# A hybrid encoder trunk: one projection of the recurrent layer and the value projection of the attention layer change their place in two order strings

## Chip, cores and metric

The kernel runs on one core of one Trainium2 chip. The metric is device time in microseconds (us); the time before is the median of three runs, 1386.49 us (1385.02 to 1387.21).

## The reference, cut to what matters

Sequence 512, width 1024, one batch, two layers. Each layer adds three blocks to x: a mixer, a cross-attention into 256 memory tokens, and a SwiGLU feed-forward network with 2816 hidden units.

```
layer 0 mixer: h = rmsnorm(x);  h @ w_in gives q, k, v, z (4 delta-rule heads) and xb, gb (512 channels)
    delta rule in chunks of 64 over q, k, v;  o = rmsnorm(o) * silu(z)
    xb = causal_conv4(xb) + b;  r, i = sigmoid(block_diag(xb));  a = exp(-8 r softplus(-l))
    hs = scan(a, sqrt(1 - a^2) * i * xb);  y_b = gelu(gb) * hs;  concat(y_a, y_b) @ w_out
layer 1 mixer: h @ w_in gives qc, kc, vc (4 differential heads, two softmaxes each), q_lat, kv_lat, k_rope
    qd, kd, vd from the latents (4 latent heads, rotary part);  both kinds of heads attend chunk-causally
    concat(yc, yd) @ w_out
```

All is float32. A product of two float32 matrices is made by three matmuls on values split into a high part and a low part (`mm3`, line 454): high times high, high times low, low times high, each in the fast float32r format. Score, transpose and probability matmuls use plain float32.

## The kernel before, in words

The activations lie transposed, 128 features by 512 positions a tile, and all 8 tiles of x stay in SBUF. Each weight tile (128 x 1024) is loaded by the SP queue into one of three raw buffers, its high part is written by ScalarE or VectorE (`wh`, line 368 or 363), its low part by VectorE (`wl`, line 385), each into one of three buffers; a projection of a 128-feature tile is then 24 matmuls of 512 columns (8 k-tiles, three products each).

The program does not issue as it is written. Every operation goes into a plan (`Plan.add`), where its rank is its place in the program plus a small bias, and `Plan.schedule` deals the operations to the engines one after another with a cost table: on each engine it takes, of those that can start within 20 ns (TensorE) or 60 ns (others) of the earliest, the one with the lowest rank. So TensorE fills every wait with something of higher rank if its operands are ready. A copy that either ScalarE or VectorE can make goes where it ends sooner. PSUM has eight banks, all under the tag `ps`; SBUF scratch has 70 slots; an operation may take a bank only when enough stay free for those of lower rank that still wait. The issue order that comes out is fixed in the program; the chip then waits on semaphores.

The ranks come from two strings. `EVEN` (line 1490) is layer 0's mixer. The letters around the change: `R` is the delta-rule recurrence (`recur`), `x0` to `x3` project and convolve the channel tiles (`xhead`, line 1038: 24 matmuls, a multiply by the norm factor into `cx`, one scale and three shifted multiply-adds into `cv`), `g0` to `g3` project the gate tiles (`ghead`, line 1044: 24 matmuls and the multiply into `gb`; gelu comes in `L`), `W` loads the block-diagonal weights, `L` (`lru`, line 1071) makes 8 float32 matmuls on the four `cv` tiles, sigmoids, the scan, gelu and the split into `ybhh`, `ybhl`, `z` are the gates of the delta-rule heads, `N` its norm, `F` the filler, which is layer 0's memory keys and values (`mem_kv`, line 645), and `Y` the last step of the delta-rule heads.

`ODD` (line 1491) is layer 1's mixer: `L` the latent projection, `K` and `Q` the key and query projections of the differential heads (`natural_heads`, line 1376: 96 matmuls into four banks, then for each of four position tiles an eviction into `xn`, a square, a sum, and after one reciprocal root a multiply), `N` the latent norm, `V` their value projection (`values`, line 1403: 96 matmuls into four banks and four evictions into `vc`, four weight tiles), `U` the up-projections of the latents (`latent_up`, line 1285), `R` the rotary part and key norms (`rope`), `D0` to `D3` the latent heads (`mla`, line 1354), `C0` to `C3` the differential heads (`diff`, line 1410), `F` layer 1's memory keys and values: 96 matmuls, in eight weight tiles of 12 matmuls each, two banks at a time. The C heads read `vc`; the D heads read `vd` of `U` and not `vc`.

Ahead of this lies layer 0's feed-forward network and behind it the output projection, which needs all eight heads.

Of the kernel before, what the change touches and what calls it, by code (L numbers as in the profile page):

```python
# [20 lines left out]
D, S, NM, FF = 1024, 512, 256, 2816  # L21
# [279 lines left out]
class Trunk:  # L301
# [465 lines left out]
    def even(self, filler):  # L767
# [333 lines left out]
        def gated(h):  # L1101
            pT = self.px()
            for t in range(4):
# [9 lines left out]
               "z": zhead, "Y": gated}  # L1113
        for name in EVEN.split():
            self.mark[name] = len(self.plan.ops)
# [115 lines left out]
    def odd(self, filler):  # L1231
# [178 lines left out]
        def diff(h):  # L1410
            ck, cq = pairT(g["od_k"], h, self.cqk[:, h:h + 1]), pairT(g["od_q"], h, 1.0)
            slope = 2.0 ** (-8.0 * (h + 1) / 4)
            P = []
            for t in range(4):
                n = 128 * (t + 1)
                sl = slice(t * 128, (t + 1) * 128)
                pr, sm = [], self.small([128, 2], "smm")
                rows = [slice(i * 64, i * 64 + 64) for i in range(2)]
                sc = [self.px()[:, :n] for _ in rows]
                self.mmpair(sc, [cq[r, sl] for r in rows], [ck[r, :n] for r in rows])  # L1420
                for i in range(2):
                    p = self.slot("P")
                    mx = self.small([128, 1], "mx")
                    self.submax(p[:, :n], sc[i], self.dist[t][:, :n], mx)
                    self.ts(mx, mx, -slope, ALU.mult)
                    self.act(p[:, :n], p[:, :n], AF.Exp, scale=slope, bias=mx, accum_out=sm[:, i:i + 1])
                    pr.append(p)
                self.recip(sm, sm)
                self.mul(sm[:, 1:2], sm[:, 1:2], self.lam)
                self.ts(pr[1][:, :n], pr[1][:, :n], sm[:, 1:2], ALU.mult)  # L1430
                self.stt(pr[0][:, :n], pr[0][:, :n], sm[:, 0:1], pr[1][:, :n], ALU.mult, ALU.subtract)
                P.append(pr[0])
            po = self.pv(P, vc, h)
            y = self.scr("yc")
            sq = self.scr("ysq")
            self.act(sq, po, AF.Square)
            cs = self.px()
            self.mm(cs, self.ones, sq)
            self.rsqrt_wide(sq, cs, 1.0 / 128, self.eps)
            self.stt(y, po, self.csub, sq, ALU.mult, ALU.mult)  # L1440
            a, b = self.pair("ych")
            self.split(a, b, y)
            yk[h] = (a, b)
# [3 lines left out]
        for i in range(4):  # L1447
            todo[f"D{i}"] = lambda i=i: mla(i)
            todo[f"C{i}"] = lambda i=i: diff(i)
        for name in ODD.split():  # L1450
            todo[name]()
# [35 lines left out]


LATE = {"norm_mix0": 30, "norm_mix1": 30, "norm_x0": 0, "norm_x1": 0, "norm_ffn0": 40, "norm_ffn1": 40, "gate": 40, "consts": 200}
EVEN = "k0 k3 k1 k2 A q3 I T0 q2 T1 T2 v1 q1 q0 T3 T4 P T5 S v2 v0 V0 V1 V2 v3 V3 R x0 g0 x3 x1 g2 g1 x2 g3 W L z0 z2 z1 N z3 F Y"  # L1490
ODD = "L K N Q V U R D3 D0 C1 C2 D1 C0 C3 D2 F"
HOLD = ("T0", "R")
NSLOT = 70
WRAW = 3
# [92 lines left out]
```

## Time and profile before

| | |
|---|---|
| median of three runs | 1386.49 us |
| the profiled execution, its time | 1383.43 us |
| its span, first to last instruction | 1381.6 us |
| granted TensorE clock over the span | 1.000 |
| TensorE matmul busy | 1369.6 us, 99% |
| TensorE weight loads busy | 1124.8 us, 81% |
| VectorE busy | 824.3 us, 60% |
| ScalarE busy | 563.0 us, 41% |

A matmul's end in the trace is modelled, and consecutive matmuls overlap, so the busy time of TensorE counts stretches as full in which the matmuls stand further apart than they need. What a stretch had to do is read from the counts of its matmuls and the distance of their starts where they stand densest.

### The profile page before, as it was taken

To read this page: it belongs to the slowest core of one execution; us is meant where nothing else is said; L and a number is where in the kernel's file an instruction comes from. 1 tells how busy PE (TensorE), PEld (TensorE's weight loads), DVE (VectorE), ACT (ScalarE), POOL (GpSimd) and SP (SyncE) were. 2 spreads that over 40 slices of the span, in tenths; PEclk is the share of its full clock that TensorE was granted. 3 is DMA by queue.
4 is the path that set the end of the run, shared out by engine and by line. 5 is a ranking of instruction groups with operands and counts; after the bars stand their busy time and mean duration, and the time that the engine had idled before them with its cause. 6 is when DMAs were issued, how large, how long until landed. Compare 5 with 4: busy or idle time off the path is not lost.

```text
span 1381.6 us, 18085 instructions
## 1 busy us (share of the span) xinstructions
PE 1369.6 (99%) x7212; PEld 1124.8 (81%) x7212; DVE 824.3 (60%) x1474; ACT 563.0 (41%) x998; POOL 3.0 (0%) x10
## 2 busy tenths in 40 slices
PE   9999999999999999999999999999999999999998
PEld 7788787888888888888889885688888888888887
DVE  7988877867744433544454469976774443344432
ACT  5763438425533222333233357843652222233221
POOL 0000000000000000000000000000000000000000
PEclk9999999999999999999999999999999999999999
DMA  6121121531232223332233220132122322422232
GB/s 241 55 86 47 48 75 35 179 95 61 76 105 92 88 90 118 125 104 83 84 101 110 96 73 31 31 135 94 46 92 92 106 70 93 128 92 92 88 107 80
DMA packets 40692, 125.89 MB, mean 91 GB/s; under 512 B 4896, under 2 KB 5536, under 8 KB 40608
## 3 DMA queue, kind: packets, MB, share of 16 engines
q1 hardware_dynamic: 40608, 124.74, 27.9%
q8 instruction: 56, 0.92, 0.3%
q14 instruction: 28, 0.23, 0.1%
HBM read 122.63 MB, written 2.10 MB: 90 GB/s over the span
## 4 chain that ended last, share of the span: by engine, by line
PE 96%; DVE 3%; ACT 1%; issue 0%; DVEq 0%
PE ps L434 91%; PE ps L440 3%; PE ps L470 2%; PE ps L450 1%; DVE gt L385 0%; ACT P L368 0%; DVE gt L418 0%; DVE cv L400 0%; DVE wl L385 0%; ACT sq L368 0%; DVE ybhl L385 0%; DVE kn L363 0%; DVE cT L365 0%; DVE kn L385 0%; ACT PT L368 0%
## 5 line engine op out<-in xcount | busy, mean ns | idle before, releaser
L368 ACT ACTIVATE wh<-wr 128x1024 fp32r<-128x1024 f32 (+3 forms) x218 | 212.3, 974 | 628.0 <-PE ps L434 421.0
L434 PE MATMUL ps<-hh,wl 128*128 128x512 f32 x960 | 375.8, 392 | 0.3 <-DVE wl L385 0.3
L434 PE MATMUL ps<-hh,wh 128*128 128x512 f32 x960 | 376.1, 392 | 0.0
L434 PE MATMUL ps<-hl,wh 128*128 128x512 f32 x960 | 375.8, 391 | 0.0
L385 DVE TENSOR_TENSOR wl<-wr,wh 128x1024 fp32r<-128x1024 f32 (+3 forms) x243 | 272.9, 1124 | 120.8 <-ACT wh L368 120.1
L434 PEld LDWEIGHTS ps<-hl,wh 128*128 128x128 f32 x960 | 180.3, 188 | 38.4 <-issue 1.5
L434 PEld LDWEIGHTS ps<-hh,wl 128*128 128x128 f32 x960 | 180.3, 188 | 38.0 <-issue 0.7
L434 PEld LDWEIGHTS ps<-hh,wh 128*128 128x128 f32 x960 | 180.2, 188 | 37.9 <-issue 0.9
L434 PE MATMUL ps<-ghh,wh 128*128 128x512 f32 x352 | 136.9, 389 | 0.0
L434 PE MATMUL ps<-ghl,wh 128*128 128x512 f32 x352 | 136.9, 389 | 0.0
L434 PE MATMUL ps<-ghh,wl 128*128 128x512 f32 x352 | 136.9, 389 | 0.0
L385 DVE TENSOR_TENSOR up<-ps,R 128x512 f32<-128x512 f32 x44 | 30.4, 691 | 139.6 <-PE ps L434 139.6
L385 DVE TENSOR_TENSOR x<-x,ps 128x512 f32<-128x512 f32 x56 | 37.9, 687 | 80.6 <-PE ps L434 80.4
L385 DVE TENSOR_TENSOR gate<-ps,R 128x512 f32<-128x512 f32 x44 | 30.4, 691 | 90.5 <-PE ps L434 89.9
L434 PEld LDWEIGHTS ps<-ghl,wh 128*128 128x128 f32 x352 | 66.1, 188 | 13.8
L434 PEld LDWEIGHTS ps<-ghh,wh 128*128 128x128 f32 x352 | 66.1, 188 | 13.8
L434 PEld LDWEIGHTS ps<-ghh,wl 128*128 128x128 f32 x352 | 66.1, 188 | 13.6
L434 PE MATMUL ps<-wh,hl 128*128 128x512 f32 (+1 forms) x128 | 49.0, 383 | 0.0
L434 PE MATMUL ps<-wl,hh 128*128 128x512 f32 (+1 forms) x128 | 48.7, 380 | 0.0
L434 PE MATMUL ps<-wh,hh 128*128 128x512 f32 (+1 forms) x128 | 48.6, 380 | 0.0
L1485 ACT ACT_TABLE_LOAD x28 | 35.9, 1283 | 1.2 <-PEq L1569 0.7
L400 DVE SCALAR_TENSOR_TENSOR cv<-cx,vcols,cv 128x511 f32<-128x511 f32 (+2 forms) x48 | 35.8, 745 | 0.3
(388 smaller groups left out, 1829.5 us busy)
## 6 DMA issues: line engine op xcount, KB each, us to landing
wr<-in_ffn_in_dram SPq DMA_DIRECT2D x88, 512.0 KB, 3.5
wr<-in_ffn_out_dram SPq DMA_DIRECT2D x32, 384.0 KB, 3.0
wr<-in_ev_in_dram SPq DMA_DIRECT2D x20, 512.0 KB, 3.5
wr<-in_ffn_out_dram SPq DMA_DIRECT2D x32, 320.0 KB, 2.8
wr<-in_xwk_dram SPq DMA_DIRECT2D x8, 512.0 KB, 3.5
wr<-in_xwv_dram SPq DMA_DIRECT2D x8, 512.0 KB, 3.7
wr<-in_ev_out_dram SPq DMA_DIRECT2D x8, 512.0 KB, 3.5
wr<-in_xwq_dram SPq DMA_DIRECT2D x8, 512.0 KB, 3.5
```

The source lines that it names most:

```text
L368: self.plan.add(ACT, lambda: self.nc.scalar.activation(out, in_, f, **k), outs, ins, self.acost(in_, len(ins) + len(outs) - 2), "tanh" if ...
L385: self.dve(lambda: self.nc.vector.tensor_tensor(out, a, b, op=op), [out], [a, b])
L400: self.dve(lambda: self.nc.vector.scalar_tensor_tensor(out, a, s, b, op0=op0, op1=op1), [out], [a, b] + sc, 1.0, len(sc))
L434: self.plan.add(PE, lambda: self.nc.tensor.matmul(ps, l, r, start=start, stop=stop, **k), [ps], [l, r], cost, None, n * (1 if l.dtype == F ...
L440: self.nc.tensor.matmul(out, l, r, start=True, stop=True)
L450: self.nc.tensor.matmul(ps[i], l[i], r[i], start=True, stop=True)
L470: self.plan.add(PE, lambda: self.nc.tensor.transpose(out, in_, i), [out], [in_, i], 109.0, None, in_.shape[0])
L1485: self.nc.scalar.preload_act_table_set(pre)
```

## The change

Two ranks move. In `EVEN`, `x2` comes ahead of `g2` and `g1` in place of behind them. In `ODD`, `V` leaves its place between `Q` and `U` and comes behind `D3` and `D0`, and `C1 C2 D1 C0 C3 D2` becomes `C1 D1 C2 D2 C0 C3`. No operation is added, removed or resized.

```
-EVEN = "... V3 R x0 g0 x3 x1 g2 g1 x2 g3 W L z0 z2 z1 N z3 F Y"
-ODD = "L K N Q V U R D3 D0 C1 C2 D1 C0 C3 D2 F"
+EVEN = "... V3 R x0 g0 x3 x1 x2 g2 g1 g3 W L z0 z2 z1 N z3 F Y"
+ODD = "L K N Q U R D3 D0 V C1 D1 C2 D2 C0 C3 F"
```

## Rows read from the trace of the kernel before

**Rows 1.** The page: busy time of each engine, and the chain that ended last by engine.
```profile
PE 1369.6 (99%) x7212; PEld 1124.8 (81%) x7212; DVE 824.3 (60%) x1474; ACT 563.0 (41%) x998; POOL 3.0 (0%) x10
PE 96%; DVE 3%; ACT 1%; issue 0%; DVEq 0%
```

**Rows 2.** The timeline of TensorE in the dense stretch of the value projection, first and last of 73 consecutive matmuls (start us, us, engine, line, operation, names, shapes, count).
```profile
799.82 0.39 PE L434 MATMUL ps<-wh,hl 128*128 128x512 f32 x1
...
816.14 0.39 PE L434 MATMUL ps<-wh,hl 128*128 128x512 f32 x1
```

**Rows 3.** The same view, where plain float32 matmuls, transposes and the paired scores of a C head stand in a run, each with the instruction behind it.
```profile
206.63 7.03 PE L434 MATMUL ps<-cv,gbd 128*128 128x512 f32 x16
...
213.72 0.40 PE L434 MATMUL ps<-hl,wh 128*128 128x512 f32 x1
...
771.52 1.47 PE L470 MATMUL ps<-consts,latn 128*128 128x128 f32 x12
772.74 0.48 PE L434 MATMUL ps<-wh,hh 128*128 128x512 f32 x1
773.06 0.39 PE L434 MATMUL ps<-wl,hh 128*128 128x512 f32 x1
...
848.23 0.70 PE L450 MATMUL ps<-cT,cT 64*128 64x256 f32 x4
848.86 0.33 PE L470 MATMUL ps<-consts,P 128*128 128x128 f32 x1
...
873.84 1.13 PE L450 MATMUL ps<-cT,cT 64*128 64x512 f32 x4
874.90 0.33 PE L470 MATMUL ps<-consts,P 128*128 128x128 f32 x1
```

**Rows 4.** Groups of TensorE instructions from 824.8 to 911.25 us: the eight heads and the filler (line, engine, operation, names, count; busy us, mean ns of one; idle before).
```profile
L470 PE MATMUL ps<-consts,P 128*128 128x128 f32 x80 | 13.7, 276 | 0.0
L434 PE MATMUL ps<-wh,mh 128*128 128x512 f32 x32 | 13.7, 433 | 0.0
L434 PE MATMUL ps<-wl,mh 128*128 128x512 f32 x32 | 13.6, 423 | 0.2 <-DVE wl L385 0.2
L450 PE MATMUL ps<-cT,cT 64*128 64x256 f32 (+3 forms) x64 | 13.3, 478 | 0.5 <-ACT PT L368 0.5
L434 PE MATMUL ps<-wh,ml 128*128 128x512 f32 x32 | 13.0, 407 | 0.0
L434 PE MATMUL ps<-dT,dT 96*128 96x128 f32 (+3 forms) x32 | 10.3, 444 | 0.3
L434 PE MATMUL ps<-PT,vd 128*128 128x512 f32 (+3 forms) x32 | 9.8, 439 | 0.0
L434 PE MATMUL ps<-PT,vc 128*128 128x512 f32 (+3 forms) x32 | 9.6, 442 | 0.2 <-DVE PT L363 0.2
L470 PE MATMUL ps<-consts,xn 128*128 128x128 f32 x32 | 4.8, 272 | 0.0
L434 PE MATMUL ps<-ysq,ones 128*128 128x512 f32 x8 | 4.3, 618 | 0.0
L470 PE MATMUL ps<-consts,kn 128*96 128x128 f32 x16 | 2.7, 278 | 0.1
L470 PE MATMUL ps<-consts,qn 128*96 128x128 f32 x16 | 2.4, 275 | 0.0
L470 PE MATMUL ps<-consts,kr 128*128 128x128 f32 x8 | 1.2, 272 | 0.0
```

**Rows 5.** Busy time of each engine in five stretches of layer 1's mixer: the end of `Q`, the rest of `V`, `U`, the rotary part, the heads (us, then busy us and count of each engine, granted clock, DMA share, GB/s).
```profile
792.70:801.00 8.30, 8.30 (x39) 6.86 (x38) 7.53 (x11) 5.83 (x10) 0.00 (x0) 1.00 0.30 93
801.00:816.30 15.30, 15.30 (x69) 12.69 (x68) 3.14 (x3) 3.77 (x6) 0.00 (x0) 1.00 0.31 104
816.30:824.80 8.50, 8.50 (x50) 7.86 (x49) 7.75 (x23) 7.48 (x19) 0.00 (x0) 1.00 0.19 64
824.80:833.80 9.00, 8.92 (x59) 6.67 (x58) 8.58 (x30) 6.97 (x17) 0.00 (x0) 1.00 0.07 15
833.80:911.25 77.45, 76.22 (x359) 50.17 (x358) 71.77 (x259) 62.19 (x166) 0.00 (x0) 1.00 0.16 54
```

**Rows 6.** The timeline of VectorE: the low parts of the filler's first three weight tiles.
```profile
817.51 1.22 DVE L385 TENSOR_TENSOR wl<-wr,wh 128x1024 fp32r<-128x1024 f32 x1
...
830.96 1.21 DVE L385 TENSOR_TENSOR wl<-wr,wh 128x1024 fp32r<-128x1024 f32 x1
...
848.34 1.21 DVE L385 TENSOR_TENSOR wl<-wr,wh 128x1024 fp32r<-128x1024 f32 x1
```

**Rows 7.** The timeline of layer 0's mixer around `x2` and the end of `L`, of VectorE, ScalarE and TensorE.
```profile
204.08 2.32 DVE L400 SCALAR_TENSOR_TENSOR cv<-cx,vcols,cv 128x511 f32<-128x511 f32 x3
...
209.49 4.15 ACT L368 ACTIVATE gt<-ps,vcols 128x512 f32<-128x512 f32 x7
...
238.79 1.21 DVE L385 TENSOR_TENSOR wl<-wr,wh 128x1024 fp32r<-128x1024 f32 x1
...
240.06 0.50 PE L434 MATMUL ps<-wl,mh 128*128 128x512 f32 x1 [1.55 <-DVE wl L385]
```

**Rows 8.** Busy time of each engine from 188 to 206 us (the projections around `x2`) and from 235 to 241 us (the end of `L`), columns as in rows 5.
```profile
188.00:206.00 18.00, 18.00 (x88) 14.77 (x87) 13.21 (x20) 7.90 (x10) 0.00 (x0) 1.00 0.25 82
235.00:241.00 6.00, 4.45 (x29) 3.54 (x28) 6.00 (x9) 4.61 (x6) 0.00 (x0) 1.00 0.02 2
```

More of the change, by code (lines that the diff above doesn't have):

```diff
@@ L1489 @@
 LATE = {"norm_mix0": 30, "norm_mix1": 30, "norm_x0": 0, "norm_x1": 0, "norm_ffn0": 40, "norm_ffn1": 40, "gate": 40, "consts": 200}
-EVEN = "k0 k3 k1 k2 A q3 I T0 q2 T1 T2 v1 q1 q0 T3 T4 P T5 S v2 v0 V0 V1 V2 v3 V3 R x0 g0 x3 x1 g2 g1 x2 g3 W L z0 z2 z1 N z3 F Y"
-ODD = "L K N Q V U R D3 D0 C1 C2 D1 C0 C3 D2 F"
+EVEN = "k0 k3 k1 k2 A q3 I T0 q2 T1 T2 v1 q1 q0 T3 T4 P T5 S v2 v0 V0 V1 V2 v3 V3 R x0 g0 x3 x1 x2 g2 g1 g3 W L z0 z2 z1 N z3 F Y"
+ODD = "L K N Q U R D3 D0 V C1 D1 C2 D2 C0 C3 F"
 HOLD = ("T0", "R")
```

## The prediction

> **What bounds the kernel now.** I read the page's busy times first: TensorE is busy 99% of the span and 96% of the chain that ended last [rows 1]. That leaves nothing to gain if it is taken at its word, so the second view is a timeline of a dense stretch, for the price of a matmul that waits for nothing: 72 steps from 799.82 to 816.14 us, 0.2267 us for a three-product matmul of 512 columns [rows 2]. Rows 3 give the others. A float32 pass of 512 columns is (213.72 - 206.63 - 0.23) / 16 = 0.429 us. A transpose is 0.109 us: 1.22 us to the next start, plus the 0.09 us by which the following matmul's step exceeds 0.227, over 12. The paired scores of a C head take 1.06 us at 512 columns and 0.63 at 256, so on a line 0.845 at 384 and 0.415 at 128, 2.95 us a head.
>
> With these I price what TensorE did from 824.8 to 911.25 us, the stretch of the eight heads [rows 4]: 152 transposes, 16.6 us; 96 filler matmuls, 21.8; three groups of 32 float32 passes (eight each of 512, 384, 256 and 128 columns, 8.58 us a group), 25.7; eight passes of `ysq`, 3.4; four C heads of pairs, 11.8; 0.2 for `U`'s last matmul. That is 79.5 us of work in 86.45 us: **6.9 us are lost** in a stretch that the windows show as almost full. Who holds it up is in the windows [rows 5]: from 833.8 us VectorE is busy 71.77 of 77.45 us and ScalarE 62.19, while TensorE's own work there is some 72 us. Two engines with the same work that wait on each other can't both be full. Just before, under `V`, VectorE had 3.14 us to do in 15.30 us. So the attention stage has its vector work crowded behind a stage that has none.
>
> The filler `F` could close the gaps, but its low parts are made by the same VectorE at the highest rank: the first at 817.51, the second at 830.96, the third at 848.34 us [rows 6], each good for 12 matmuls, 2.7 us. The filler starves when it is wanted.
>
> A rule of the Trainium skill speaks on how much is lost. "Perfetto Trace Analysis", "Identifying the Most-Contended Engine", says that matmul busy time does not tell the distance from the roofline and that the busy share of weight loads does. The trace agrees with its first half. By its second half, loads run at 12.69/15.30 = 83% under `V` and 50.17/77.45 = 65% under the heads [rows 5], so 17 us would be lost there. A float32 pass of 0.429 us has one load as a matmul of 0.227 us has, so I keep 6.9.
>
> **The change part by part.** No instruction is added; what counts is what lies beside what.
>
> `V` behind `D3 D0`. Its 96 matmuls (21.8 us) and four evictions no longer lie under `Q`'s end but beside the heads. First, what loses its cover: `Q`'s evictions, squares and sums. In the old order they ran under `V` without a gap. Now `U` follows directly. VectorE and ScalarE have 7.53 + 5.83 us at `Q`'s end, 7.75 + 7.48 in `U`, 8.58 + 6.97 in the rotary part [rows 5], 44.1 us, 22.1 on each if evenly dealt. So the heads' scores come at 792.7 + 22.1 = 815 us in place of 834. In those 22.1 us TensorE has 0.9 us of `Q`, 8.5 of `U` and 7.2 of the first transposes and scores (9.0 less 1.8 of filler): 16.6, and 5.5 us are empty unless `V` fills them. One of its four weight tiles does so (24 x 0.2267 = 5.4 us), if it has been split. The split has a rank behind `U`, `R`, `D3` and `D0`. Rows 6 say both: the filler's first tile was let through 1.2 us into `U`, its second 6 us after `U`. The ends are 0 and 5.5 us; I take 1.7, nearer to the first tile.
>
> Second, what gains cover: the heads. VectorE's 71.8 us there become 75.4 with three of `V`'s low parts (1.21 us each, rows 6), and TensorE's 72 become 88.4 with three quarters of `V` (16.3 us). VectorE's share falls from 93% to 85%. At 13.21/18.00 = 73% the projections of layer 0 lost nothing [rows 8]; at 93% the heads lost 5.4 of 77.45 us, 7%. An even line gives 4% at 85%, 3.7 us; waiting grows faster than evenly towards full, so I take half, 1.9 us. Ends 0 and 5.4. `V`'s rank is ahead of the C heads, so its splits wait only for `D3` and `D0`, and each brings 5.4 us where one of the filler brings 2.7. `F` is left over at the end, when VectorE is free; the output projection needs all heads, and the last of the filler covers the tail of `C3`, as it now covers `D2`'s.
>
> On the SP queue `V`'s four loads stand behind those of `U`; the DMA engines are 30% busy there and under 20% later [rows 5], so I cost that at nothing. If a raw buffer came late, it would add to the hole above. The order of the C and D heads alternates now; the same work, nothing.
>
> Sum for this part: 6.9 lost before, 1.7 + 1.9 = 3.6 after, **3.3 us less**.
>
> `x2` ahead of `g2 g1`. The eight float32 matmuls of `L` start at 206.63 us, right behind the last 512-column matmul of `g3` [rows 3]; `x2`'s last shifted adds end at 204.08 + 2.32 = 206.40 us [rows 7], just in time. With `x2` 10.9 us earlier (two projections), that slack is 11 us, but `g3` is still the projection ahead of `L` and has the lower rank, so `L` starts where it did, and the chain of sigmoids from 209.49 us on, which ScalarE sets, stays. `x2`'s vector work stays inside a stretch where VectorE has 4.8 of 18 us free [rows 8]. What could be gained is at the end of `L`: VectorE is full from 235 to 241 us [rows 8], and the filler's low part at 238.79 makes TensorE wait 1.55 us [rows 7]. Ends: -1.55 us if the gap closes, +1 us (estimate: one VectorE delay of that low part's length, 1.2 us) if it grows. I take 0: nothing in the chain that ends there has moved.
>
> The profiled execution took 1383.43 us, the median of the runs is 1386.49, 3.06 above. 1383.43 - 3.3 = 1380.1 on its scale, **1383.2 us** on the median's.
>
> **The rivals.**
> 1. The hole takes back what the heads gain. For it: `Q`'s end and `U` together keep both vector engines full, and rows 6 show 6 and 17 us of waiting for later splits. Against it: the first tile got through. 5.5 + 1.9 = 7.4 lost, +0.5: 1387.0.
> 2. Slower: `V` straddles the heads. Its sums run over all four weight tiles, so from its first matmul to its evictions it holds four of eight PSUM banks, where the filler held two. If its second tile is split only behind `D0`'s softmax, the heads run on four banks for some 50 us. Price: twice the present 7% over 51 us, 7.0, and the full hole, 5.5: 12.5 - 6.9 = +5.6, 1392.1. It decides at 10 us of straddling (5.5 + 0.138 x 10 = 6.9). Against it: `V`'s rank is ahead of every C head's, and it asks for only three more splits.
>    The clock would add to this. "TensorE: Matmul & The Clock Gate", "HAM oscillation", says that idle gaps of the engine take its clock to half. The granted clock is 1.00, 2.4 GHz, in every window of rows 5 and 8, the 1.55 us gap among them; a longer gap no row shows.
> 3. Both parts at their good end: heads fed throughout, and the 1.55 us gap closed: 6.9 - 0.2 + 1.55 = 8.2 less, 1378.3; half-way from the forecast 1380.7.
> 4. The change does not do what it says: the planner picks by readiness first, and with `V`'s tiles split early it would issue `V` right behind `Q` as now. Then 1386.5. Against it: `U`'s weights are then next in the three buffers, and `U` has the lower rank.
>
> **How the numbers follow.** Forecast 0.48 (its own range 1380.8 to 1385.5, by hole 0.5 to 3 and heads 0.5 to 3.5), rival 1 0.24, rival 2 0.12, rival 3 0.12, rival 4 0.04. A difference of 0.2%, 2.8 us, is about what a measurement of this kernel can tell from none: 1383.7 and 1389.3 are the limits. Of the forecast 0.36 lies below 1383.7 and 0.12 above; rival 3 adds 0.12 to faster; of rival 1 0.20, of rival 2 0.03 and rival 4 are the same; the rest is slower. Faster 0.48, same 0.39, slower 0.13. The range 1379.5 to 1388.5 leaves out most of rival 2 and the good end of rival 3.
>
> **What would show it.** Right: the first scores of `D3` some 19 us nearer to the end of `Q`; `V`'s matmuls in single runs between transposes and scores; VectorE at 80 to 88% over the heads; a dense run of filler matmuls of 10 us or more at their end; the same table of prices gives 3 to 5 us lost. Wrong: TensorE idle by name behind `U`, waiting for a low part (rival 1); `vc` evicted more than 45 us after `Q`'s last matmul, and scores waiting for banks (rival 2); `V` ahead of `U` (rival 4). In layer 0 the wait before 240 us should stand at 1 to 2 us; if it is gone, that part was worth it.

## The result and the profile after

The changed kernel takes 1393.63 us (median of 4 runs, 1393.36 to 1394.9) where the kernel before takes 1385.76 beside it (4 runs): a ratio of 1.0060, 95% interval 1.0048 to 1.0072. It is 7.9 us **slower**, 0.6%; the forecast was 3.3 us faster.

The profiled execution took 1394.9 us, 11.5 more than that of before. Its page shows the same work, and the two lines that answer to [rows 1] hardly differ, so the page alone doesn't show where the time went:

```profile
PE 1377.1 (99%) x7212; PEld 1131.5 (81%) x7212; DVE 822.6 (59%) x1469; ACT 564.6 (41%) x1001; POOL 3.0 (0%) x10
PE 95%; DVE 4%; ACT 1%; issue 0%; DVEq 0%
```

The windows of layer 1's mixer, with the columns of [rows 5], show the place. The stretches are `U`; from `U`'s last matmul to `D3`'s scores; `V` beside `D3` and `D0`; `V` alone; the other heads.

```profile
797.67:806.35 8.68, 8.68 (x50) 8.03 (x49) 8.67 (x17) 8.44 (x24) 0.00 (x0) 1.00 0.00 0
806.35:819.60 13.25, 11.84 (x51) 8.43 (x50) 9.71 (x35) 9.48 (x21) 0.00 (x0) 0.74 0.35 110
819.60:838.57 18.97, 18.97 (x91) 13.78 (x90) 12.08 (x49) 10.12 (x27) 0.00 (x0) 1.00 0.10 35
838.57:849.80 11.23, 11.23 (x53) 9.29 (x51) 3.65 (x4) 3.23 (x5) 0.00 (x0) 1.00 0.28 89
849.80:903.00 53.20, 48.94 (x238) 30.42 (x237) 47.72 (x197) 42.87 (x124) 0.00 (x0) 1.00 0.03 12
```

Read down: behind `U` TensorE has 51 instructions in 13.25 us, is idle 1.41 us, and its mean granted clock is 0.74 of 2.4 GHz, so part of it ran at 1.2; every window of [rows 5] had 1.00. Then, from 838.57 us, 11 us in which TensorE is full and both vector engines idle; then 53 us in which TensorE is idle for 4.26.

With the prediction's prices (a matmul's price summed over all that start in a stretch, against the time to the next start), 6.7 us are lost from 800 to 820 us and 9.0 from 820 to 920, 15.7 in all. Before it was 0.1 and 7.3. That is 8.2 us of the 11.5. The rest: behind `L` in layer 0 the clock is 0.51 for 3.5 us, 1.7 us lost, and the first 150 us lose another 1.7, with one such stretch near 58 us; the profiled execution of e5, below, has both without the new recurrence, so they are not the change's (last section). Price table and clock together account for the whole difference of the two profiled executions.

Why the stretch behind `U` is thin is seen in the timeline of VectorE. First the rotary part, then `V`'s low parts:

```profile
810.38 0.49 DVE L385 TENSOR_TENSOR kn<-kr,rsq 128x128 f32<-128x128 f32 x2
...
812.00 0.36 DVE L385 TENSOR_TENSOR qn<-rt,rt 128x64 f32<-128x64 f32 x2
812.27 1.23 DVE L385 TENSOR_TENSOR wl<-wr,wh 128x1024 fp32r<-128x1024 f32 x1
813.40 0.23 DVE L385 TENSOR_TENSOR qn<-rt,rt 128x64 f32<-128x64 f32 x1
813.54 2.36 DVE L385 TENSOR_TENSOR wl<-wr,wh 128x1024 fp32r<-128x1024 f32 x2
```

and TensorE, from `Q`'s last matmul (797.67) and `U`'s last (806.12) on:

```profile
797.67 0.39 PE L434 MATMUL ps<-wh,hl 128*128 128x512 f32 x1
...
806.12 0.39 PE L434 MATMUL ps<-wh,lthl 128*128 128x512 f32 x1
...
808.35 0.48 PE L434 MATMUL ps<-wh,hh 128*128 128x512 f32 x1
...
809.65 0.52 PE L470 MATMUL ps<-consts,kn 128*96 128x128 f32 x2 [0.61 <-DVE kn L385]
810.73 0.52 PE L470 MATMUL ps<-consts,kn 128*96 128x128 f32 x2 [0.56 <-DVE kn L385]
...
811.81 0.98 PE L434 MATMUL ps<-wh,hh 128*128 128x512 f32 x2
...
815.66 0.63 PE L434 MATMUL ps<-wl,hh 128*128 128x512 f32 x1
816.09 0.63 PE L434 MATMUL ps<-wh,hl 128*128 128x512 f32 x1
...
819.29 2.50 PE L434 MATMUL ps<-dT,dT 96*128 96x128 f32 x8
```

In the kernel before, `Q`'s last matmul (the one ahead of `V`'s 96, the last of which starts at 816.14 us [rows 2]) and the first scores of `D3`:

```profile
794.38 0.39 PE L434 MATMUL ps<-wh,hl 128*128 128x512 f32 x1
...
833.28 0.49 PE L434 MATMUL ps<-dT,dT 96*128 96x128 f32 x2
```

`V`'s first matmul comes at 808.35, but only the first product of a sum, high part times high part, runs before the low part `wl` is there, at 813.5 us. In between stand short transposes, and the waits that the trace names there are for VectorE's rotary work (`kn`, `qn`). At 815.66 the step from one 512-column matmul to the next is 0.43 us in place of 0.2267: the clock's lower level. `D3`'s first scores come at 819.29, 21.6 us behind `Q`'s end; before they came at 833.28, 38.9 us behind it.

The end of `V`, on ScalarE and on TensorE:

```profile
848.17 2.73 ACT L368 ACTIVATE vc<-ps,rn 128x512 f32<-128x512 f32 x4 [2.34 <-PE ps L434]
```

```profile
813.59 1.12 PE L450 MATMUL ps<-cT,cT 64*128 64x128 f32 x4
...
850.11 2.21 PE L450 MATMUL ps<-cT,cT 64*128 64x256 f32 x12
```

`C1`'s first score pair runs at 813.59 and the next at 850.11, behind the last of `V`. Whether the planner kept the next pair back for its rank or for want of a bank, the trace doesn't show. What ends TensorE's waits from 849 to 903 us is VectorE's softmax (us in total, times, longest):

```profile
PE ps L470 <- DVE P L400: 2.7, 3, 1.3
PE ps L470 <- DVE mx L415: 0.9, 1, 0.9
```

And the filler is not there to fill these waits. Its first matmul comes only 24 us behind `V`, and 25 of its 96 matmuls lie ahead of the heads' last probability matmul, where the kernel before had 68:

```profile
873.63 0.47 PE L434 MATMUL ps<-wh,mh 128*128 128x512 f32 x1
```

### The profile page after: what moved, and what is told of

Read it like the earlier page. It is cut to its first block, busy times and chain, and to the rows that moved or that the text cites. A ratio compares the mean times of both kernels' runs of the same rounds, so it can differ in the third digit from the quotient of the medians.

```text
span 1393.1 us, 18097 instructions
## 1 busy us (share of the span) xinstructions
PE 1377.1 (99%) x7212; PEld 1131.5 (81%) x7212; DVE 822.6 (59%) x1469; ACT 564.6 (41%) x1001; POOL 3.0 (0%) x10
## 4 chain that ended last, share of the span: by engine, by line
PE 95%; DVE 4%; ACT 1%; issue 0%; DVEq 0%
PE ps L434 90%; PE ps L440 3%; PE ps L470 2%; DVE P L415 1%; DVE P L400 0%; DVE gt L385 0%; DVE gt L418 0%; DVE cv L400 0%; DVE P L396 0%; PE ps L450 0%; ACT wh L368 0%; ACT sq L368 0%; DVE ybhl L385 0%; DVE wl L385 0%; DVE kn L363 0%
## 5 line engine op out<-in xcount | busy, mean ns | idle before, releaser
L400 DVE SCALAR_TENSOR_TENSOR hl<-x,vcols,hh 128x512 fp32r<-128x512 f32 x48 | 34.9, 747 | 0.0
```

The costliest lines, as they stand in the source:

```text
L400: self.dve(lambda: self.nc.vector.scalar_tensor_tensor(out, a, s, b, op0=op0, op1=op1), [out], [a, b] + sc, 1.0, len(sc))
```

## The experiments

Sixteen kernels ran, 5 to 12 runs each, in four groups (e1 to e4, e5 to e8, e9 to e12, e13 to e16). Each group ran beside the kernel before, whose medians were 1386.0, 1385.6, 1385.2 and 1386.3 us; where two kernels of different groups are compared, their ratios to it are the safer measure. The line of the changed kernel and the first line of the table are from the result above. "Lost" is the price table's loss in the profiled execution from 800 to 820 us (the hole) and from 820 to 920 us (the heads); a profiled execution is one run, and where its clock fell the loss has that in it.

| kernel | median us | ratio to before, 95% | hole | heads |
|---|---|---|---|---|
| before | 1385.8 | 1 | 0.1 | 7.3 |
| the change | 1393.6 | 1.0060 (1.0048 to 1.0072) | 6.7 | 9.0 |
| e1 recurrence alone | 1385.5 | 0.9998 (0.9988 to 1.0008) | 0.1 | 7.3 |
| e2 odd layer alone | 1393.5 | 1.0061 (1.0045 to 1.0076) | 6.6 | 9.0 |
| e3 V's place, old heads | 1392.6 | 1.0048 (1.0035 to 1.0062) | 7.1 | 7.7 |
| e4 heads' order alone | 1388.3 | 1.0014 (1.0005 to 1.0022) | 0.1 | 10.3 |
| e5 e3, V split early | 1385.4 | 1.0004 (0.9995 to 1.0013) | 0.3 | 7.2 |
| e6 e3, V's matmuls late | 1395.9 | 1.0077 (1.0063 to 1.0091) | 8.3 | 10.7 |
| e7 both | 1386.3 | 1.0004 (0.9995 to 1.0014) | 0.6 | 6.7 |
| e8 V ahead of the rotary part | 1390.8 | 1.0035 (1.0022 to 1.0047) | 1.9 | 8.6 |
| e9 before, filler split early | 1383.6 | 0.9985 (0.9976 to 0.9994) | 0.0 | 5.4 |
| e10 the change, V split early | 1380.5 | 0.9963 (0.9949 to 0.9977) | 0.3 | 2.5 |
| e11 e7, filler split early | 1383.4 | 0.9985 (0.9976 to 0.9994) | 0.7 | 5.0 |
| e12 e3, hole filled with repeats | 1391.7 | 1.0042 (1.0030 to 1.0055) | 1.9 | 7.7 |
| e13 e10, old recurrence | 1380.2 | 0.9965 (0.9952 to 0.9977) | 0.3 | 2.5 |
| e14 the change, first tile early | 1383.7 | 0.9985 (0.9976 to 0.9993) | 0.9 | 4.0 |
| e15 the change, splits behind U | 1387.4 | 1.0014 (1.0005 to 1.0023) | 0.7 | 10.1 |
| e16 e10, filler split early | 1381.7 | 0.9976 (0.9965 to 0.9987) | 0.3 | 3.9 |

**Which edit.** The change taken apart. e1:

```
-EVEN = "... x0 g0 x3 x1 g2 g1 x2 g3 W L ..."
+EVEN = "... x0 g0 x3 x1 x2 g2 g1 g3 W L ..."
```

> Only the recurrence's x2 goes ahead of g2 g1; the odd layer as before. Theory A (the whole loss of 7.9 us is the value projection's place): within 2 us of before, 1384 to 1388, with at most one half-clock stretch of 3.4 us near 243 us, behind L, worth 1.7. Theory B (the recurrence's part gives a good share of the loss, by the clock behind L): 1388 or more.

e2, with the recurrence as before:

```
-ODD = "L K N Q V U R D3 D0 C1 C2 D1 C0 C3 D2 F"
+ODD = "L K N Q U R D3 D0 V C1 D1 C2 D2 C0 C3 F"
```

> Only the odd layer's new order; the recurrence as before. Theory A: 1391.5 to 1394, the clock at half for some 6.8 us behind U, and the value projection's last 50 matmuls in one run of 11 us. Theory B: under 1391.

e3, only `V` moved:

```
+ODD = "L K N Q U R D3 D0 V C1 C2 D1 C0 C3 D2 F"
```

> V behind D3 D0, but the heads behind it in their old order C1 C2 D1 C0 C3 D2. If V's place alone does it: slower than before by 5 us or more, 1391 to 1396, with the same hole behind U. If the alternating order of C and D heads does it: within 2 us of before.

e4, only the heads:

```
+ODD = "L K N Q V U R D3 D0 C1 D1 C2 D2 C0 C3 F"
```

> V in its old place behind Q, the heads alternating D3 D0 C1 D1 C2 D2 C0 C3. If V's place alone does it: within 2 us of before, 1384 to 1388. If the order of the heads does it: slower by 5 us or more.

The recurrence is worth nothing, `V`'s place 0.48%, 6.6 us, and the order of the heads 0.14%, 2.2 us, by itself; e2 has both and the whole loss. So theory A is nearly right, but the order of the heads has a price too. Where, e4's timeline of TensorE shows, with the window behind it:

```profile
864.65 0.55 PE L470 MATMUL ps<-consts,P 128*128 128x128 f32 x3 [1.68 <-DVE P L396]
```

```profile
864.65:870.16 5.51, 5.50 (x18) 3.43 (x19) 3.70 (x13) 2.11 (x7) 0.00 (x0) 0.69 0.00 0
```

One wait of 1.68 us for a softmax, and a clock of 0.69 over the 5.5 us from there on, which is 1.7 of the 3.0 us that the heads lose more than before.

**What about V's place.** Three theories: A, the hole behind `U`, since `V`'s low parts rank behind the rotary work; B, the run of `V` alone, since `V` ranks ahead of the C heads; C, the four PSUM banks of the prediction's second rival. e5 changes only the ranks of `V`'s splits, on e3:

```
-                hi, lo = self.wload(A[key][q], 2 * n)
+                raw, hi, lo = self.wraw(A[key][q], 2 * n)
+                if key == "od_v":
+                    self.plan.bias = self.at["U" if q == 0 else "R"] - len(self.plan.ops)
+                self.split(hi[:, :2 * n], lo[:, :2 * n], raw[:, :2 * n])
+                self.plan.bias = 0
...
         for name in ODD.split():
+            self.at[name] = len(self.plan.ops)
             todo[name]()
```

> As e3 (V behind D3 D0, old order of heads, 1392.6 us), but the splits of V's weight tiles take an early rank: the first tile's that of U, the others' that of the rotary part. V's matmuls keep their rank. Theory A (the hole behind U is the whole loss: V's low parts wait behind the rotary work on VectorE, and the clock then falls): the hole of 7.1 us and the half clock are gone, 1384 to 1387.5. Theory B (the run of V alone, while the vector engines idle and the C heads wait, costs as much as the hole): 1388 to 1391. Theory C (V's four PSUM banks starve the heads): within 2 us of e3, since the banks are held as long.

e6 changes only the rank of its matmuls, on e3:

```
+                        self.plan.bias = 130 if key == "od_v" else 0
                         self.mm3(ps[t][:, :n], (hT[k][0][:, sl], hT[k][1][:, sl]), w, k == 0, k == 7)
+                        self.plan.bias = 0
```

> As e3, but V's matmuls rank 130 places lower, behind the scores of the first two C heads; the splits keep their rank. Theory A: the hole stays, 1390.5 to 1394.5. Theory B: the run of some 50 V matmuls is broken up, the heads are fed, 1387 to 1390. Theory C: V holds its banks longer, slower than e3 by 2 us or more.

e7 has both edits:

> Early splits of e5 and low-ranked matmuls of e6 together. Theory A: within 1.5 us of e5. Theory B: faster than e5 by 2 us or more, 1380 to 1385. Theory C: slower than e5 by 2 us or more.

e8 puts `V` between `U` and `R`:

```
+ODD = "L K N Q U V R D3 D0 C1 C2 D1 C0 C3 D2 F"
```

> V between U and the rotary part, heads in their old order: its splits no longer stand behind the rotary work, and its 93 matmuls run in one piece while the vector engines do that work. Theory A: no hole, 1383 to 1386.5. Theory B: the heads' vector work comes behind one long run of V, as in the kernel before: 1385 to 1388.

e5 is back at the time of before, 7.1 us under e3 (6.1 by the ratios), with the hole gone from 7.1 to 0.3 us: theory A. Its heads lose 7.2 us, as before: with the heads in their old order, `V` beside them gains nothing there. Theory B falls: with `V`'s matmuls ranked lower e6 is 3.3 us slower than e3, and on top of e5 the same edit (e7) changes nothing. Nor do four held banks cost by themselves. In e5 `V` holds its four from 806.45 us until its evictions,

```profile
839.26 2.74 ACT L368 ACTIVATE vc<-ps,rn 128x512 f32<-128x512 f32 x4
```

and the window over that time has no idle TensorE (0.4 us lost by the prices):

```profile
806.45:842.00 35.55, 35.55 (x174) 27.65 (x173) 25.53 (x85) 18.39 (x42) 0.00 (x0) 1.00 0.23 74
```

In the changed kernel they are held for some 40 us up to the evictions, in e5 for 33 and in e6 for 48; in e6 the hole grew as well, so its loss can't be put down to banks alone, and no run holds the banks longer with all else equal. e8 missed: 1390.8, where A gave 1383 to 1386.5. Its profiled execution is the fastest of its runs (1386.5), so the trace accounts for only some 3 us of the 5. The clock goes with the rest: the profiled run had a mean of 0.999, the other five 0.995 to 0.997, and they took 1388.5 to 1392.0, some 1.2 us more for each 0.001. In which stretch it fell is not known.

**Is the filler's lateness the heads' loss?** In e9, on the kernel before (and in e11 and e16), the filler's first four weight tiles get an earlier rank (`self.at` is filled as in e5):

```
-                hi, lo = self.wload(A[key][l, q], 1024)
+                raw, hi, lo = self.wraw(A[key][l, q], 1024)
+                if l == 1 and 4 * (key == "xwv") + q < 4:
+                    self.plan.bias = self.at["C1"] - len(self.plan.ops)
+                self.split(hi, lo, raw)
+                self.plan.bias = 0
```

> The kernel before, with one thing new: the splits of the filler's first four weight tiles take the rank of the first C head, so that VectorE makes the low parts before the heads crowd it. If the heads' loss of 6.9 us is the filler coming late: 3 to 5 us faster, 1381 to 1383. If the heads are bound by their own vector work: within 1.5 us of before.

> e7 (V behind D3 D0 with early splits and low-ranked matmuls) with the filler's early splits of e9. If the filler's lateness is the heads' loss: 1382 to 1384, faster than e7 by 2 us or more. If the heads are bound by their own vector work: within 1.5 us of e7, 1385 to 1387.5.

e9 gains 0.15%, 2.1 us of 1385, between the two theories, and the heads' loss falls from 7.3 to 5.4 us. e11 is 2.8 us under e7 (2.6 by the ratios), as the filler theory had it, and its heads lose 5.0 us in place of 6.7. So by the price table the filler's lateness is about a quarter of the heads' loss in these kernels.

**The change with its hole closed.** e10 is the changed kernel with the early splits of e5:

> The changed kernel as it is (new recurrence, V behind D3 D0, alternating heads), with the early splits of V's weight tiles of e5. If the hole behind U is what the change costs: 1393.6 less 6 to 8, 1385.5 to 1387.5, with the two vector engines still idle under the run of V. If the order of the heads costs 1 to 2 us by itself, as e4 and e2 against e3 say, it stays above e5: 1386.5 to 1388.

1380.5 us, 0.37% faster than before and 13.1 us under the changed kernel: more than either theory said. e13 takes the recurrence's edit out of it again, so that e5 and e13 differ by the order of the heads alone:

> e10 (the changed kernel with V's splits early, 1380.5 us) with the old order of the recurrence. If the 4.9 us between e5 and e10 come from the alternating heads: as e10 within 1 us, 1379.5 to 1381.5. If from the recurrence: as e5, 1384.5 to 1386.5.

1380.2: all of the 4.9 to 5.2 us between e5 and these two (5.4 to 5.7 by the ratios) is the heads' order, which cost 2.2 us with `V` in its old place. e13's VectorE and TensorE behind `U`:

```profile
806.99 2.36 DVE L385 TENSOR_TENSOR wl<-wr,wh 128x1024 fp32r<-128x1024 f32 x2
811.20 1.23 DVE L385 TENSOR_TENSOR wl<-wr,wh 128x1024 fp32r<-128x1024 f32 x1
```

```profile
804.21 0.40 PE L434 MATMUL ps<-wh,lthl 128*128 128x512 f32 x1
804.44 0.39 PE L434 MATMUL ps<-wh,hh 128*128 128x512 f32 x1
804.67 0.39 PE L434 MATMUL ps<-wl,hh 128*128 128x512 f32 x1
...
810.81 0.39 PE L434 MATMUL ps<-wl,hh 128*128 128x512 f32 x1
811.04 0.60 PE L470 MATMUL ps<-consts,kn 128*96 128x128 f32 x4
```

`V`'s matmuls, low parts included, follow `U`'s last within 0.23 us and run for 6.6 us without a gap while VectorE does the rotary work. The windows of `V` and of the heads behind it:

```profile
804.44:840.00 35.56, 35.56 (x174) 27.64 (x173) 25.52 (x85) 18.41 (x42) 0.00 (x0) 1.00 0.22 74
840.00:900.00 60.00, 60.00 (x305) 40.27 (x304) 55.88 (x212) 50.48 (x137) 0.00 (x0) 1.00 0.17 54
```

By the profile TensorE is never idle, though VectorE is busy 55.88/60 = 93% of the second; the prices give 0.4 and 2.1 us lost. The filler starts early here, and all 96 of its matmuls lie ahead of the heads' last probability matmul:

```profile
845.28 0.81 PE L434 MATMUL ps<-wh,mh 128*128 128x512 f32 x1
```

In e5 it is 62 of them. That goes with the losses (e10, e13 and e16: 96 matmuls, 2.5 to 3.9 us; the changed kernel and e2: 25, 9.0), but it is no law: e4 has 74 and loses 10.3. Why the plan deals the filler so differently is not shown.

**How early.** e14 and e15 change e10's ranks: only the first tile at `U`'s rank (the others keep their own), or all four at `R`'s.

```
-                    self.plan.bias = self.at["U" if q == 0 else "R"] - len(self.plan.ops)
+                    self.plan.bias = self.at["U" if q == 0 else "V"] - len(self.plan.ops)
```

> The changed kernel with only the first weight tile of V split early, at U's rank; the other three stay behind D3 D0. The prediction held that one tile (5.4 us of matmuls) fills the stretch behind U. If that is so: within 2 us of e10, 1380 to 1383. If the second tile too must be there before the rotary work ends: a hole of 2 to 4 us comes back behind the first, 1384 to 1390.

```
-                    self.plan.bias = self.at["U" if q == 0 else "R"] - len(self.plan.ops)
+                    self.plan.bias = self.at["R" if q == 0 else "R"] - len(self.plan.ops)
```

> The changed kernel with all four splits of V at the rank of the rotary part's first step: ahead of the rotary work, but behind U's evictions. If being ahead of the rotary work is what counts: as e10 within 2 us, 1379 to 1383. If V's first low part must be ready by U's last matmul: a hole of 1 to 3 us, 1383 to 1387.

One early tile brings 10 of the 13 us: 1383.7, just between the two cases. Its second tile's low part then comes 0.32 us late, and that is all of the hole that names VectorE:

```profile
812.67 0.50 PE L434 MATMUL ps<-wl,hh 128*128 128x512 f32 x1 [0.32 <-DVE wl L385]
```

e15 closes the hole too (0.7 us) but is 6.9 us slower than e10, outside the first theory and 0.4 us above the second, and not by a hole: its loss, 10.1 us, lies under the heads, where the clock is at half for 6.8 us behind a dip of TensorE:

```profile
845.00:849.00 4.00, 3.25 (x16) 1.34 (x13) 4.00 (x18) 3.90 (x15) 0.00 (x0) 1.00 0.01 2
849.00:855.80 6.80, 6.65 (x15) 3.72 (x15) 6.13 (x34) 5.16 (x17) 0.00 (x0) 0.51 0.00 0
```

That is 3.4 of the 10.1 us. As in the changed kernel only 25 filler matmuls lie under the heads, though `V`'s last matmul stands at 840.94 us here, as early as in e5. So a closed hole and an early `V` are not enough for the heads; why this plan serves them badly is open.

e16 is e10 with e9's lines:

> e10 with the filler's early splits of e9. If the 2.6 us still lost under the heads are the filler's lateness: 1378.5 to 1380. If not: within 1 us of e10, or slower where the earlier splits push the heads' vector work back, 1380 to 1383.

1381.7, no gain (1.8 us slower by the ratios, with intervals that overlap): what e10 still loses is not the filler's lateness.

**What the half clock costs.** e12 repeats the first matmul of each of `V`'s sums in e3:

```
+        def go():
+            for i in range(again):
+                self.nc.tensor.matmul(ps, l, r, start=start, stop=stop or i < again - 1, **k)
...
-  self.mm3(ps[t][:, :n], ..., w, k == 0, k == 7)
+  self.mm3(ps[t][:, :n], ..., w, k == 0, k == 7, 6 if key == "od_v" else 1)
```

> e3 with the first matmul of each of V's four sums issued six times instead of once: 20 more matmuls (4.5 us at the full clock) in the hole behind U, in the same order otherwise; the sums are unchanged. It asks what the half clock costs in the hole. If the idle time is free and the clock is what the hole costs: the clock stays at full, 1389 to 1391.5. If the clock adds little to the idle time: 1392 to 1397, by what of the 4.5 us is not hidden.

The same window in e3 and in e12:

```profile
803.56:818.90 15.34, 13.84 (x57) 9.70 (x56) 11.04 (x44) 10.76 (x25) 0.00 (x0) 0.78 0.32 103
```

```profile
803.56:818.90 15.34, 14.77 (x80) 11.14 (x78) 11.80 (x49) 11.42 (x28) 0.00 (x0) 1.00 0.32 103
```

With 20 matmuls more in it TensorE is through this stretch no later (the same matmul of `V` starts at 818.53 in e12 and at 818.91 in e3), and its clock stays at 1.00. e3's mean clock of 0.78 over 15.34 us is 3.4 us of lost clock (0.22 x 15.34), and the added work is 4.5 us: the clock pays for three quarters of it, idle time, down from 1.50 to 0.57 us, for most of the rest. So the half clock is about half of the hole's 7.1 us, as far as this pair of profiled executions shows. The median is 0.9 us under e3's, 0.2 above the first theory's range, and the two intervals overlap: a gain in time is not shown.

## Why the prediction failed

**V behind D3 D0, first the hole: the step that failed.** The prediction put 1.7 us here, between 0 and 5.5, because in [rows 6] the filler's first low part was let through 1.2 us into `U`. It is 6.7. The row was read out of its place: in the kernel before, the stretch ahead of that `U` is `V`'s, where VectorE is busy 3.14 of 15.30 us [rows 5]. The filler's first split is the first thing that VectorE does behind that idle stretch; it had waited 3.60 us for TensorE:

```profile
816.57 0.69 DVE L363 CAST wh<-wr 128x1024 fp32r<-128x1024 f32 x1 [3.60 <-PE ps L434]
```

In the new order `Q`'s end stands there, VectorE is full (8.67 of 8.68 us in `U`), and a split that ranks behind `U`, `R`, `D3` and `D0` waits until the rotary work is nearly done, at 812.27 us. The prediction's own sum had said this: 44.1 us of work for two engines at once. That the rank of the splits is the cause is shown by e10, which changes nothing else and loses 0.3 us there. That one tile would fill the stretch was right: e14 gives it that tile in time, and its hole is 0.9 us. That e14 takes 1383.7 us, where the forecast was 1383.2, is in part luck: its heads lose 4.0 us where 1.9 was forecast.

**The upper end was too low as well.** 5.5 us was idle time at the full clock. Behind `U` the clock fell, 3.4 us of the 6.7. The working itself has slips that nearly cancel: `Q`'s last matmul starts at 794.38 us, so `Q` has 1.9 us in the sum and not 0.9, and of the 8.5 and 7.2 us counted as work 1.5 were already lost by the prices. With both, 6.0 us stood empty and not 5.5. From 833.8 us on the heads lost 6.0 us by the prices and not 5.4. The prediction cited the rule of the Trainium skill, "TensorE: Matmul & The Clock Gate", "HAM oscillation", for the second rival alone and put no number on it; the trace agrees in that the clock fell where TensorE was short of work, 0.74 over 13.25 us, but no long gap was needed: the longest idle time that the trace names there is 0.61 us.

**Second, the heads.** 1.9 us of loss was forecast, 0 to 5.4; it is 9.0. With the splits early it is 2.5 (e10, e13) and 4.0 with one early tile (e14), so the size could nearly be had, but only with the heads alternating: in the old order it is 7.2 (e5). In the changed kernel 50 of `V`'s 96 matmuls stand behind `D0`, from 838.57 to 849.80 us, the vector engines are nearly idle beside them, and the other heads come behind, at first without filler. That the rank of the splits sets this loss too is shown by e10; that the late run of `V` is the way it does so is argued, and e15, which has no such run and loses 10.1, speaks against it as the only way. And the law behind the number is wrong: a loss that follows VectorE's share. In e13 VectorE is 93% busy over 60 us, as it was in [rows 5], and TensorE loses 2.1 us by prices, where the prediction's 7% would be 4.2. What the traces show to differ is what TensorE has at hand: all of the filler in e13, a quarter of it in the changed kernel.

**The order of the heads** was put at nothing. It costs 2.2 us alone, 0.9 with `V` late (e2 against e3, where the intervals overlap), and brings some 5 with `V` in time (e13 against e5). That its sign turns is shown; why is not. The plan fixes TensorE's order before the run, and the traces only say where its waits fall.

**The recurrence** was right at nothing: e1 is at 0.9998, and the wait that the prediction said would stand at 1 to 2 us, 1.55 in [rows 7], is 1.54 in the changed kernel:

```profile
241.78 0.50 PE L434 MATMUL ps<-wl,mh 128*128 128x512 f32 x1 [1.54 <-DVE wl L385]
```

**The rivals.** The second, at 0.12, came closest with 1392.1: a full hole of 5.5 us and 7.0 us lost in the heads, with the clock said to come on top; 6.7 and 9.0 were measured, the clock within the 6.7. Its sign was there too: `vc` evicted at 848.17 us, 50.5 behind `Q`'s last matmul. But its reason, four banks of eight, is not shown: e5 holds them for 33 us without loss, the other half of its sign, scores that wait for banks, is in no wait of the trace, and what the banks cost at 40 us stays open. The first rival had the hole and no more. The range ended at 1388.5 because it left out "most of rival 2", the only case with both terms high; both come back to one thing, splits that rank behind a VectorE that is full (e10), and the sum gave each a mild value of its own.

**The signs to look for** did their work in part: the scores of `D3` 17.3 us nearer to `Q`'s end, where some 19 were forecast, and the run of filler at the end, from 905 us on; neither says that time was gained. The run of filler is no good sign: in e10 and e13 the last filler matmul stands ahead of the heads' last probability matmul. The other signs of a right forecast failed: `V` in single runs (50 of its matmuls stand in one run), VectorE at 80 to 88% over the heads (63.46/83.40 = 76% from 819.60 to 903.00 us), and 3 to 5 us lost (15.7). Behind `U` TensorE was idle for the rotary work's `kn` and `qn` by name, not for a low part as rival 1 had it. The rule of the page "Perfetto Trace Analysis" of the Trainium skill, "Identifying the Most-Contended Engine", would have had weight loads at 40.27/60 = 67% in e13's heads mean 11.5 us of loss, against the same 83% as in the prediction; the prices give 2.1, so leaving it out of the sum was right.

## What to carry to other kernels

When a stage is moved to cover a gap, check when its own preparation can run, on the engine that makes the gap: here a few lines that rank the weight splits early turned 7.9 us of loss into 5 us of gain, with the order of the heads that the change brought. A row that shows such preparation getting through counts only if the same engine is as free in the new place. Where TensorE runs short of work for a stretch, allow for the clock beside the empty time: behind `U` it was 3.4 of 6.7 us. And look whether the filler is used up under the stage that needs it: the changed kernel has a dense run of it left over at the end, the three fastest, e10, e13 and e16, have none.

## What the runs showed of the hardware

The granted clock decides most of the spread between runs of one kernel. Of 21 runs of the kernel before beside e1 to e4, one at a mean clock of 1.000 took 1383.53 us, one at 0.998 took 1385.08, one at 0.997 took 1386.4 and one at 0.996 took 1388.7: some 1.2 us for each 0.001. A straight line of that slope takes up 85% of the variance of 20 of the 21; the other lists a clock of 0.949 at 1386.93 us and doesn't fit. So 0.3% of a kernel's time comes and goes with the clock.

The same thin stretch does not always bring the clock down. Behind `L`, TensorE is busy 4.45 of 6.00 us before [rows 8] and nearly the same in the changed kernel, where the clock then falls and in before it does not:

```profile
236.70:242.70 6.00, 4.46 (x29) 3.53 (x28) 6.00 (x9) 4.60 (x7) 0.00 (x0) 1.00 0.00 0
242.70:246.20 3.50, 3.50 (x11) 2.83 (x11) 3.27 (x5) 2.70 (x6) 0.00 (x0) 0.51 1.00 281
```

e2 and e4, with the old recurrence, show the fall at this place in their profiled executions, e1 with the new one and e3 with the old one do not. What decides it there is not shown. Behind `U` the profiled executions of the changed kernel, e2, e3 and e6 all show it, with 1.4 to 1.5 us of idle time in 13 to 15 where it was counted.
